# Another order for the weight splits and sums of a hybrid decoder layer: each behind the preceding split or sum alone, a room of its own for one sum, ten halves for a sum made ahead

## The chip, the cores and the metric

The kernel runs on one core of a Trainium2 chip. The metric is the device time of one execution in microseconds. Five engines work side by side, each through its own list of instructions in order: TensorE (PE, with its weight loads PEld), VectorE (DVE), ScalarE (ACT), GpSimd (POOL) and SyncE (SP, which here only starts transfers). They wait for each other through semaphores. Transfers between device memory and on-chip memory run on 16 DMA engines, which all queues share.

## The reference

The program is one decoder layer over 256 tokens with a width of 2048, all in float32. A recurrent branch and an attention branch are merged by gates (the "mix"), projected, normalised and added; then comes an MLP with a squared ReLU. The part on which this change works is the end:

```python
x = x + rmsnorm(mix @ w_out[l], norm_mix_post[l])
h = rmsnorm(x, norm_mlp_pre[l])
u = jnp.square(jax.nn.relu(h @ w_mlp_up[l]))      # 2048 -> 8192
x = x + rmsnorm(u @ w_mlp_down[l], norm_mlp_post[l])  # 8192 -> 2048
```

## The kernel before, in words

**Split weights.** A float32 product is made of three products of a shorter format: each operand is a high part plus a low part, and high x high, high x low and low x high are added. All weights are streamed once, in halves of 128 x 1024 elements (512 KB). The class `Stream` numbers them j = 8, 9, ... and takes care of three steps for each: SP loads the raw half (`wraw`, a ring of four, and every fifth half into `xraw`), ACT copies it into the high part `whi` (L108), DVE subtracts that from the raw half to get the low part `wlo` (L109). `ws.ahead` keeps the splits 6 halves ahead of PE (`AHEAD`), and the rings of `whi` and `wlo` hold 6. A ring slot of raw halves comes free only when its split is done, so DVE's order also decides when SP may load.

**The stages.** In order of time: the projections of the recurrent and the attention branch; the mix stage, whose groups alternate between a quarter of the gate (g) and a quarter of the recurrent projection (rp0 to rp3); the output projection; then twice (f = 0, 1, each half of the inner width) an up stage and two down passes (n = 0, 1, each 1024 output columns). At the end of rp0 to rp3 DVE merges the gate and both branches (L918, L919), after which PE transposes the result (L901).

**The down projection with seven products.** A down pass runs through 16 pairs of halves. For most of them (`SEVENS`) a 2 x 2 block product is made with seven block products instead of eight. Three of the seven need sums of weight blocks: `right_sums` makes them from halves a and b in three DVE instructions, L59 (T1 and T3, 1024 columns), L61 (T2, written over half of b) and L62 (T4, 512 columns). Each of T1, T3, T4 is split as well: `thi` on ACT (L154), `tlo` on DVE (L155). PE's products are all on L1191. The partial results stand in PSUM banks (s, dQ, dP, dCs). At the end of the sevens of a pass ACT and DVE combine them into four quarters (L1240 to L1244); then the last two pairs are added by plain products, and `finish` evacuates each quarter: for f = 0 by a DVE add (L1326) and a store that ACT issues (`acc_away`, L1327); for f = 1 it adds what was stored, and the last pass goes on to the norm and the output (L1366 to L1385).

**Sums made ahead.** DVE has no room for all sums in the down passes, so some are made earlier. `sums_ahead` loads a pair with four POOL transfers into `early` (L365), makes its three sums on DVE in the same three instructions, and stores them with three POOL transfers (`away`, L374); a later pass loads them back (`second`, L138). It is a generator that advances by one step for each half that PE begins, and its three gaps say how many halves pass between the loads, ahead of the sums, and between the stores. Six sums are made in the mix stage with the gaps (1, 2, 1), which is 4 + 2 + 3 = 9 halves each; eight more in the two up stages and the passes beside them.

**What sets the order.** The program is written in one stream, and a scheduler orders each engine's instructions by its own model of when they become ready. Two devices hold it: `ws.ahead`, by where it is called, and `ws.keep`. An instruction handed to `ws.keep` (all splits of pairs in the down passes, their sums and the splits of these) was given `tc.keep_in_program_order`, which keeps it behind everything that was written before it for the same engine. At the start of a new pass, the splits and sums of the first pairs are written behind the `finish` of the pass before.

**Rooms.** `pc`, `pb`, `po`, `pa` and `const` are pools of on-chip memory with different lifetimes. T1 and T3 live in a tile `t`, T4 in one of the four tiles of `u2`, a ring that the activations of the up stage and the four quarters at the end of a pass use too.

## Time and profile before

| | before |
|---|---|
| device time, median of 3 runs | 1503.71 us (1503.61 to 1503.78) |
| the profiled execution's own time | 1503.92 us |
| its span in the profile | 1502.2 us |
| granted TensorE clock, mean over the span | 0.995 |
| PE busy | 1483.7 us, 99% |
| DVE busy | 1143.2 us, 76% |
| ACT busy | 852.3 us, 57% |
| POOL busy | 77.6 us, 5% |
| read from and written to device memory | 316.38 MB, 24.64 MB |

A row of the timeline reads: start in us, duration, engine, line, operation, what is written <- what is read, and in brackets how long the engine stood idle just before and what it waited for. "SPq" and "ACTq" are the issues of transfers. A row of the windows gives the stretch, and for each engine its busy time and, in brackets, the number of instructions begun; then the granted clock of TensorE, the mean busy share of the DMA engines and the GB/s. In the chain of waits a row gives start, duration and what ran.

### The profile page before, as it was taken

What the parts mean: (1) busy time and instruction counts of PE and PEld (TensorE: products, weight loads), DVE (VectorE), ACT (ScalarE), POOL (GpSimd) and SP (SyncE); (2) the same over time, 40 slices, a digit from 0 to 9 for tenths busy, and PEclk for the clock granted to TensorE, in tenths of its full rate; (3) what the DMA queues carried; (4) which work ended last, traced back from release to release, by engine and by line L of the source; (5) the groups of instructions that cost most, each with busy time, mean ns of one, the idle gap of its engine ahead of it and who ended that gap; (6) DMA issues with size and microseconds to landing.
All of it is one profiled execution on the core that took longest, in us unless ns stands there. A gap on an engine that the chain in (4) does not pass through costs nothing.

```text
span 1502.2 us, 20543 instructions
## 1 busy us (share of the span) xinstructions
PE 1483.7 (99%) x7556; PEld 1255.6 (84%) x7556; DVE 1143.2 (76%) x1503; ACT 852.3 (57%) x1236; POOL 77.6 (5%) x149
## 2 busy tenths in 40 slices
PE   9999999999999999999999999999899999999997
PEld 8887778888889888788889888888788888888886
DVE  6676668759578966665757987799797777799897
ACT  8564564647467664444345665566465555566463
POOL 0000000000000002020000111000110111000000
PEclk9999999999999999999999999999999999999999
DMA  9754544555646658876874887668598777677584
GB/s 339 231 167 135 185 156 139 174 191 182 201 161 200 218 174 283 296 264 242 303 240 162 317 294 255 196 214 282 176 312 283 255 258 250 201 272 270 188 273 175
DMA packets 96901, 342.38 MB, mean 228 GB/s; under 512 B 11552, under 2 KB 11808, under 8 KB 95776
## 3 DMA queue, kind: packets, MB, share of 16 engines
q1 hardware_dynamic: 80352, 288.89, 57.2%
q0 software_dynamic: 12992, 44.05, 8.2%
q10 hardware_dynamic: 3456, 8.13, 1.4%
q8 instruction: 59, 0.97, 0.3%
q14 instruction: 42, 0.34, 0.1%
HBM read 316.38 MB, written 24.64 MB: 227 GB/s over the span
## 4 chain that ended last, share of the span: by engine, by line
PE 91%; DVE 4%; DMA 2%; ACT 2%; issue 1%; DVEq 0%; ACTq 0%
PE ps L296 21%; PE ps L294 11%; PE dQ L1191 7%; PE s L1191 6%; PE dP L1191 4%; PE pp L338 3%; PE pp L334 3%; PE pp L336 3%; PE g L334 3%; PE g L338 3%; PE g L336 3%; PE dCs L1191 2%; PE q L334 2%; PE q L338 2%; PE q L336 2%; PE o L336 2%
## 5 line engine op out<-in xcount | busy, mean ns | idle before, releaser
L108 ACT CAST whi<-wraw 128x1024 fp32r<-128x1024 f32 x469 | 489.3, 1051 | 464.2 <-PE ps L296 95.4
L109 DVE TENSOR_TENSOR wlo<-wraw,whi 128x1024 fp32r<-128x1024 f32 x469 | 566.8, 1220 | 243.4 <-ACT whi L108 235.2
L296 PE MATMUL ps<-h2T,whi 128*128 128x512 f32 x960 | 223.9, 390 | 0.0
L296 PEld LDWEIGHTS ps<-h2T,whi 128*128 128x128 f32 x960 | 178.2, 188 | 35.6
L294 PEld LDWEIGHTS ps<-h2T,wlo 128*128 128x128 f32 x960 | 119.1, 192 | 2.3
L296 PE MATMUL ps<-hT,whi 128*128 128x512 f32 x512 | 120.6, 391 | 0.0
L294 PE MATMUL ps<-h2T,wlo 128*128 128x256 f32 x960 | 119.9, 283 | 0.0
L296 PEld LDWEIGHTS ps<-hT,whi 128*128 128x128 f32 x512 | 94.7, 188 | 19.5 <-issue 0.7
L1191 PE MATMUL dQ<-whi,uT 128*128 128x512 f32 (+1 forms) x284 | 104.0, 385 | 0.0
L334 PE MATMUL g<-whi,hT 128*128 128x512 f32 x256 | 101.7, 397 | 0.0
L336 PE MATMUL g<-wlo,hT 128*128 128x512 f32 x256 | 100.5, 392 | 0.0
L338 PE MATMUL g<-whi,hT 128*128 128x512 f32 x256 | 100.4, 392 | 0.0
L365 POOL DMA_DIRECT2D early<-in_w_dn x56 | 30.4, 543 | 709.0 <-DVE px L324 497.9
L108 ACT CAST whi<-xraw 128x1024 fp32r<-128x1024 f32 x47 | 49.3, 1050 | 30.6 <-PE ps L296 15.2
L294 PEld LDWEIGHTS ps<-hT,wlo 128*128 128x128 f32 x512 | 63.7, 191 | 2.1 <-issue 0.8
L109 DVE TENSOR_TENSOR wlo<-xraw,whi 128x1024 fp32r<-128x1024 f32 x47 | 57.3, 1220 | 9.8 <-ACT whi L108 9.6
L294 PE MATMUL ps<-hT,wlo 128*128 128x256 f32 x512 | 64.6, 283 | 0.0
L1191 PEld LDWEIGHTS dQ<-whi,uT 128*128 128x128 f32 x284 | 53.0, 188 | 10.9 <-DVE t L1267 0.2
L1191 PE MATMUL s<-thi,uT 128*128 128x512 f32 x152 | 54.1, 397 | 4.3 <-ACT thi L154 4.3
L334 PEld LDWEIGHTS g<-whi,hT 128*128 128x128 f32 x256 | 48.5, 189 | 10.7 <-issue 1.0
L338 PEld LDWEIGHTS g<-whi,hT 128*128 128x128 f32 x256 | 48.5, 189 | 10.3
L336 PEld LDWEIGHTS g<-wlo,hT 128*128 128x128 f32 x256 | 48.4, 189 | 9.7
(309 smaller groups left out, 2750.8 us busy)
## 6 DMA issues: line engine op xcount, KB each, us to landing
wraw<-in_w_up SPq DMA_DIRECT2D x106, 512.0 KB, 4.9
wraw<-in_w_dn SPq DMA_DIRECT2D x93, 512.0 KB, 5.4
wraw<-in_w_g SPq DMA_DIRECT2D x64, 512.0 KB, 4.7
wraw<-in_w_xy SPq DMA_DIRECT2D x64, 512.0 KB, 3.7
wraw<-in_w_q SPq DMA_DIRECT2D x32, 512.0 KB, 3.8
wraw<-in_w_ap SPq DMA_DIRECT2D x32, 512.0 KB, 3.8
wraw<-in_w_rp SPq DMA_DIRECT2D x32, 512.0 KB, 5.6
wraw<-in_w_out SPq DMA_DIRECT2D x32, 512.0 KB, 4.5
```

What stands on the lines that cost most here:

```text
L108: self.pin(self.nc.scalar.copy(hi, src))
L109: self.latest_low = self.pin(self.nc.vector.tensor_tensor(lo, src, hi.bitcast(F32), ALU.subtract))
L294: mm(ps[:, f, 1, :], w, a[:, 0, :], start=False, stop=j == 1 and k == 7)
L296: mm(ps[:, f].rearrange("p a b -> p (a b)"), w, a.rearrange("p a b -> p (a b)"), start=kt == 0, stop=j == 3 and k == 7)
L334: mm(banks[tb][n], a[:, 0, t], hi[:, n * 512 : n * 512 + 512], start=first, stop=False)
L336: mm(banks[tb][n], a[:, 0, t], lo[:, n * 512 : n * 512 + 512], start=False, stop=False)
L338: mm(banks[tb][n], a[:, 1, t], hi[:, n * 512 : n * 512 + 512], start=False, stop=last)
L365: nc.gpsimd.dma_start(w[:, quarter(i)], chunks[c][:, quarter(i)])
L1191: mm(b, a[x], w[y], start=not begun and i == 0, stop=tail and i == 2, skip_group_check=shared)
```

## The change

Three edits and two small ones that make room:

1. `ws.keep` becomes `behind_latest`: a kept split or sum is ordered only behind the latest kept one on the same engine. It is no longer held behind other instructions that were written before it.
2. T4 gets a tile of its own, `t512`, in the pool `pc`, instead of one from the ring `u2`; T1 and T3 are now in `t1024`. For this `tiny` moves from `const` to `pa` and `dg` from `pb` to `po`.
3. The six sums of the mix stage take the gaps (1, 3, 1): ten halves each.

```diff
-    tiny = const.tile([P, 194], F32, name="tiny")
+    tiny = pa.tile([P, 194], F32, name="tiny")
...
-    pin = ws.pin = ws.keep = tc.keep_in_program_order
+    pin = ws.pin = tc.keep_in_program_order
+    latest = {}
+
+    def behind_latest(i):
+
+        engine = i.ins.engine
+        if engine in latest:
+            tc.add_manual_dep(i.ins, latest[engine],
+                              mybir.DependencyInfo(mybir.DependencyClass.NoSync, mybir.DependencyReason.DATA),
+                              reason="behind_latest")
+        latest[engine] = i.ins.name
+        return i
+
+    ws.keep = behind_latest
...
-    ws.side += [sums_ahead(c, (1, 2, 1), unit_rooms) for c in summed[:6]]
+    ws.side += [sums_ahead(c, (1, 3, 1), unit_rooms) for c in summed[:6]]
...
-                dg = pb.tile([P, P], F32, name=f"dg{tb}")
+                dg = po.tile([P, P], F32, name=f"dg{tb}")
...
-                ws.sums_rooms = lambda: [pc.tile([P, 1024], F32, tag="t", name="t"), u2("t4")]
+                ws.sums_rooms = lambda: [pc.tile([P, n], F32, tag=f"t{n}", name=f"t{n}") for n in (1024, 512)]
```

The changed kernel has 13 lines more, so L1326 of before is L1339 of after, and so on from line 443.

**First place: DVE in the mix stage, at the merge of rp0.** Before; the first row is L59 of the second sum made ahead, the splits are those of the last halves of rp0 and the first of the next gate quarter:

```order
L59 TENSOR_TENSOR early_t<-early 128x1024
L109 TENSOR_TENSOR wlo_5284<-wraw_5206,whi_5283 128x1024
L61 TENSOR_TENSOR early<-early_t,early 128x512
L62 TENSOR_TENSOR early_t<-early 128x512
L109 TENSOR_TENSOR wlo_5303<-wraw_5225,whi_5302 128x1024
L109 TENSOR_TENSOR wlo_5322<-wraw_5249,whi_5321 128x1024
L109 TENSOR_TENSOR wlo_5341<-wraw_5267,whi_5340 128x1024
L109 TENSOR_TENSOR wlo_5359<-wraw_5287,whi_5358 128x1024
L109 TENSOR_TENSOR wlo_5377<-wraw_5306,whi_5376 128x1024
L918 SCALAR_TENSOR_TENSOR g_4972<-g_4972,pp 128x512
L918 SCALAR_TENSOR_TENSOR g_4974<-g_4974,pp 128x512
L919 TENSOR_TENSOR g_4972<-g_4972,m_429 128x512
```

After, from the last splits before the merge:

```order
L109 TENSOR_TENSOR wlo_5340<-wraw_5267,whi_5339 128x1024
L109 TENSOR_TENSOR wlo_5359<-wraw_5285,whi_5358 128x1024
L109 TENSOR_TENSOR wlo_5377<-wraw_5305,whi_5376 128x1024
L931 SCALAR_TENSOR_TENSOR g_4972<-g_4972,pp 128x512
L931 SCALAR_TENSOR_TENSOR g_4974<-g_4974,pp 128x512
L932 TENSOR_TENSOR g_4972<-g_4972,m_429 128x512
L932 TENSOR_TENSOR g_4974<-g_4974,m_429 128x512
L109 TENSOR_TENSOR wlo_5400<-wraw_5324,whi_5399 128x1024
L109 TENSOR_TENSOR wlo_5418<-wraw_5343,whi_5417 128x1024
L59 TENSOR_TENSOR early_t<-early 128x1024
```

The second sum stands behind the merge now, and its stores and the next sum's loads stand later on POOL accordingly.

**Second place: DVE at the boundary between the two down passes of f = 0.** Before; s, dQ, dP and dCs are the banks of the ending pass, wraw_9313 and wraw_9295 the raw halves of the first pair of the next:

```order
L1243 TENSOR_TENSOR t<-t,s_8774 128x512
L1244 TENSOR_TENSOR t<-t,s_8774 128x512
L1326 TENSOR_TENSOR t<-dQ_8776,t 128x512
L1326 TENSOR_TENSOR t<-dP_8775,t 128x512
L1326 TENSOR_TENSOR t<-dQ_8777,t 128x512
L1326 TENSOR_TENSOR t<-dCs,t 128x512
L59 TENSOR_TENSOR t<-wraw_9313,wraw_9295 128x1024
L61 TENSOR_TENSOR wraw_9313<-t,wraw_9295 128x512
L62 TENSOR_TENSOR t_9465<-wraw_9313 128x512
L109 TENSOR_TENSOR wlo_9470<-wraw_9295,whi_9469 128x1024
```

After:

```order
L59 TENSOR_TENSOR t_9464<-wraw_9313,wraw_9295 128x1024
L1254 TENSOR_TENSOR t<-s_8773,t 128x512
L61 TENSOR_TENSOR wraw_9313<-t_9464,wraw_9295 128x512
L1255 TENSOR_TENSOR t<-s_8774,t 128x512
L62 TENSOR_TENSOR t_9465<-wraw_9313 128x512
L1256 TENSOR_TENSOR t<-t,s_8774 128x512
L1257 TENSOR_TENSOR t<-t,s_8774 128x512
L109 TENSOR_TENSOR wlo_9470<-wraw_9295,whi_9469 128x1024
L1339 TENSOR_TENSOR t<-dQ_8776,t 128x512
L109 TENSOR_TENSOR wlo_9474<-wraw_9313,whi_9473 128x1024
L155 TENSOR_TENSOR tlo<-t_9464,thi 128x512
L1339 TENSOR_TENSOR t<-dP_8775,t 128x512
```

The sum of the new pass and its splits moved ahead of and between the combinations and evacuations of the old one; the other two splits of sums, a further L59 and the last two evacuations follow in the same mixed way. On ACT the first copy of the new pass moved likewise from behind the four stores of L1327 to ahead of them.

**Third place: DVE at the end of the last pass.** Before, the last two splits:

```order
L1338 TENSOR_TENSOR t<-t,acc_11918 128x512
L1338 TENSOR_TENSOR t<-t,acc_11919 128x512
L1338 TENSOR_TENSOR t<-t,acc_11918 128x512
L109 TENSOR_TENSOR wlo_13246<-wraw_13133,whi_13245 128x1024
L109 TENSOR_TENSOR wlo_13250<-wraw_13176,whi_13249 128x1024
L1366 TENSOR_TENSOR acc_11918<-dQ_12659,t 128x512
```

After:

```order
L109 TENSOR_TENSOR wlo_13246<-wraw_13133,whi_13245 128x1024
L1254 TENSOR_TENSOR t<-s_12655,t 128x512
L109 TENSOR_TENSOR wlo_13250<-wraw_13176,whi_13249 128x1024
L1255 TENSOR_TENSOR t<-s_12656,t 128x512
L1351 TENSOR_TENSOR t<-t,acc_11919 128x512
```

One split stands ahead of all the combinations now, the other behind the first of them.

## The prediction

> **What bounds the kernel now.** I read the shares of the page first, then who waited for whom on PE.

> ```profile
> PE 1483.7 (99%) x7556; PEld 1255.6 (84%) x7556; DVE 1143.2 (76%) x1503; ACT 852.3 (57%) x1236; POOL 77.6 (5%) x149
> PE s L1191 <- ACT thi L154: 4.3, 1, 4.3
> PE ptr L901 <- DVE g L919: 3.6, 1, 3.6
> PE warm L440 <- DVE ones L424: 1.1, 1, 1.1
> PE s L1191 <- DVE tlo L155: 0.5, 1, 0.5
> ```

> TensorE is the bound: 99% busy. The change removes no matmul, so it can win only where PE stands still or runs slowly. Only two waits exceed 1.1 us: 3.6 before the transposes at L901 (mix stage) and 4.3 before a product of thi at L1191 (second down pass of f = 0). Both cost more than their idle time. In windows of 2 us the columns are PE busy, granted clock, DMA share, GB/s:

> ```profile
> 606.08 0.66 PE L901 MATMUL ptr<-ident,g 128*128 128x128 f32 x4 [3.61 <-DVE g L919]
> 606.00:608.00 2.00, 1.92 (x8) 0.68 0.93 367
> 608.00:610.00 2.00, 2.00 (x6) 0.50 0.76 260
> 610.00:612.00 2.00, 2.00 (x10) 0.96 0.94 332
> 1068.00:1070.00 2.00, 0.32 (x1) 0.50 0.00 0
> 1070.00:1072.00 2.00, 2.00 (x5) 0.50 0.52 145
> 1072.00:1074.00 2.00, 2.00 (x6) 0.50 0.85 260
> 1074.00:1076.00 2.00, 2.00 (x10) 0.91 0.30 123
> ```

> After each stall PE runs at half clock for some microseconds. Stall 1: 2 x (0.32 + 0.50 + 0.04) = 1.7, with the 3.6 idle **5.3 us**. Stall 2: 0.32 x 0.50 + 2 x (0.50 + 0.50 + 0.09) = 2.3, with 4.3 and the 0.5 for tlo 7.1. A second way to it is the length of the two passes, from the chain of waits:

> ```profile
> 984.78 1.36 PE s L1191 x6
> 1062.68 2.73 PE dCs L1191 x12
> 1150.57 2.72 PE dCs L1191 x12
> ```

> The first pass lasts 984.78 to 1065.41 = 80.6, the second 1065.41 to 1153.29 = 87.9. Both run the same products, so the stall costs **7.3 us**; I take this. [...]

> **Why PE waited the first time.** Rows of DVE, ACT and POOL in order of time, then the load from the chain:

> ```profile
> 588.09 1.23 DVE L59 TENSOR_TENSOR early_t<-early 128x1024 f32<-128x1024 f32 x1 [2.88 <-DMA early<-in_w_dn]
> 592.90 2.21 POOL L365 DMA_DIRECT2D early<-in_w_dn  x4 [0.18 <-issue]
> 592.94 8.88 DMA wraw<-in_w_g
> wraw<-in_w_g SPq DMA_DIRECT2D x64, 512.0 KB, 4.7
> 601.92 1.05 ACT L108 CAST whi<-wraw 128x1024 fp32r<-128x1024 f32 x1 [4.21 <-DMA wraw<-in_w_g]
> 603.00 1.23 DVE L109 TENSOR_TENSOR wlo<-wraw,whi 128x1024 fp32r<-128x1024 f32 x1 [4.04 <-ACT whi L108]
> 604.14 1.28 DVE L918 SCALAR_TENSOR_TENSOR g<-g,pp 128x512 f32<-128x512 f32 x2
> 605.34 1.28 DVE L919 TENSOR_TENSOR g<-g,m 128x512 f32<-128x512 f32 x2
> ```

> The transposes need the merge L918/L919. It stands on DVE behind a split whose raw half took 8.88 us to arrive, against a median of 4.7. Two things delayed that half. DVE had waited 2.88 us at 588.09 for the data of a sum made ahead, so ring slots came free late; and POOL put the four loads of the next sum on the DMA engines at 592.90, in the same moment as the late half, with this sum's stores just ahead.

> ```profile
> 580.00:600.00 20.00, 20.00 (x90) 16.57 (x89) 11.81 (x12) 9.02 (x10) 5.76 (x11) 1.00 0.90 309
> 600.00:620.00 20.00, 16.39 (x70) 13.15 (x70) 14.42 (x16) 8.60 (x10) 3.47 (x7) 0.91 0.91 326
> 700.00:720.00 20.00, 20.00 (x96) 16.40 (x95) 12.60 (x14) 8.95 (x10) 0.00 (x0) 1.00 0.64 221
> ```

> **Part 1, ten halves.** The gap (1,2,1) -> (1,3,1) lets each sum take ten halves instead of nine. On DVE the second sum's L59 goes from ahead of six splits before the merge to the third place behind it; its stores and the next loads follow on POOL. Before the merge DVE loses one L59 (1.23), one L61 and one L62 (0.69 each, L61's shape as in the L1326 rows below) and the wait of 2.88: about 5.5 us. The late half is then asked for some 3 to 4 us earlier and without 1.25 MB of stores and 1 MB of loads beside it. If it takes the 4.7, the merge ends near 599.5 (an estimate: half at 594 to 595, split and casts 2.3, merge 2.6). PE's last matmul before the wait ended at 606.08 - 3.61 = 602.5, so the margin is about 3 us. Gain between 0 (half still late) and 5.3; I take 5.3, since 3 us of margin covers most of the 8.88 - 4.7 = 4.2 of lateness even if it recurs. The moved traffic, some 2.25 MB, lands in 600 to 622 on top of 326 GB/s; the next merge lies at about 640, behind a quiet stretch, and the sums further back fall near 700, where the DMA share was 0.64.

> **Part 2, the order of splits and sums.** Rows at the boundary of the passes:

> ```profile
> 1044.92 0.33 SPq L86 DMA_DIRECT2D wraw<-in_w_dn  x1
> 1050.77 20.56 SPq L86 DMA_DIRECT2D wraw<-in_w_dn  x4
> 1049.52 2.58 DVE L109 TENSOR_TENSOR wlo<-wraw,whi 128x1024 fp32r<-128x1024 f32 x2 [0.37 <-ACT whi L108]
> 1057.27 0.69 DVE L1326 TENSOR_TENSOR t<-dQ,t 128x512 f32<-128x512 f32 x1 [1.33 <-PE dQ L1191]
> 1065.43 0.69 DVE L1326 TENSOR_TENSOR t<-dCs,t 128x512 f32<-128x512 f32 x1 [2.03 <-PE dCs L1191]
> 1066.04 1.22 DVE L59 TENSOR_TENSOR t<-wraw,wraw 128x1024 f32<-128x1024 f32 x1
> 1066.53 1.04 ACT L108 CAST whi<-wraw 128x1024 fp32r<-128x1024 f32 x1 [13.42 <-DVE t L1326]
> 1085.47 6.93 DMA wraw<-in_w_dn
> ```

> The sum L59 of the next pass's first pair stood behind four evacuations, which wait for PE to end the pass; ACT's first copy waited 13.42 us behind the stores of those evacuations. PE reached 1065.4 with nothing split. After, a kept split or sum is bound only to the kept one before it. DVE's work to the first pair's last tlo is then 3 instructions of 1024 columns (1.22) and 11 of 512 (0.69), the four combinations and two evacuations among them: 3.7 + 7.6 = 11.3 us from 1049.52 + 2.58 = 1052.1, so at most 1063.4. PE comes at 1065.4, so 2 us are left over. The inputs are there: half 369 was issued at 1044.92, and the slowest down load of the chain took 6.93. Ring slots come free earlier too, where SP's four issues took 20.56 us before, and that removes the 0.5 at tlo, whose load was the late one of 1085.47. The price is that evacuations now stand behind splits. The one wanted first is dQ of the quarter (0,0), whose bank the third product of the new pass writes, 6 matmuls x 0.227 (2.72 / 12) = 1.4 us after 1065.4. By the same count DVE reaches it at 1063.4 + 1.22 and is done 0.69 later, at 1065.3: 1.5 us are left, so I count nothing, and 0.7 if DVE were 2 us later than counted. Gain 0 to 7.3; I take 7.3, as the pass before it, which starts with splits in hand, loses nothing. The boundary of f = 1 showed no wait before, and keeps at most 1.2 us (one split) in either direction; I count it at nothing, the end of its pass being hidden under PE.

> **Part 3, the end.** The last two splits pass eight small DVE instructions, so PE's dQ products need not be put off:

> ```profile
> 1485.58 0.47 PE dQ L1191 x2
> 1492.52 0.61 DVE acc L1366
> 1494.64 0.34 DVE acc L1366
> 1493.50 0.28 PE L1191 MATMUL s<-whi,uT 128*128 128x256 f32 x1
> ```

> The chain leaves PE at 1486.05 and stays on DVE and ACT to the last accumulation at 1494.64, while PE ends at 1493.78. With dQ complete some 3 us earlier DVE catches up and the tail hangs on PE: 1494.64 - 1493.78 = 0.86 less an issue, **0.75** (bounds 0 and 0.86).

> **Part 4, rooms.** A room of its own for the third sum frees u2; `tiny` and `dg` only change pools. No row shows a wait on them; nothing. One raw load early in the up stage moves behind four others on SP; its half is needed over 15 us later: nothing, or at worst one wait of a load, 6.9 less the lead.

> **Sum.** Against the profiled execution's 1503.92: 1503.92 - 5.3 - 7.3 - 0.75 = 1490.6. The median of the runs is 0.2 lower, which I leave to the thin margin named under rival C: **1490.6 us**.

> **The rivals.** *B, stall 1 moves.* The traffic of the sums is moved, not removed; a merge or the first group of rp1 to rp3 may meet a late half instead. For it: 0.90 DMA share over 40 us. Against it: DVE is busy 12 to 14 of 20 us there, so it catches up after a late half if no merge stands right behind it. Price 5.3: 1495.9.

> *C, DVE becomes the bound in places.*

> ```profile
> 1100.00:1120.00 20.00, 20.00 (x90) 16.57 (x89) 19.93 (x24) 15.06 (x21) 1.62 (x3) 1.00 0.84 292
> ```

> In a down pass DVE is busy 19.93 of 20 us, so whatever it does at a boundary is paid for later. The second pair of the new pass needs its first tlo after the 21 matmuls of the first pair and 12 of its own that use plain splits, at 1065.4 + 33 x 0.227 = 1072.9; DVE reaches it, counted on from 1063.4 (at full durations) with five of 1.22 and five of 0.69, at 1072.95. By the steps between neighbours (603.00 to 604.14, 1.14; 1065.43 to 1066.04, 0.61) both counts end some 2 us earlier. So the margin is 2.0 to -0.1. Three or four waits of up to 1 us give 1493.5.

> *D, slower.* A kept sum now stands on DVE and ACT ahead of evacuations; if its raw half is late, everything behind it in the engine's queue waits, and PE with it for a bank, as L918 stood ready behind a split that waited 4.04. [...] A late load as at 1085.47 gives a stall of some 4.3 idle and 2.3 at half clock, 6.6. It decides from the third such place on (2 x 6.6 is what is gained): three boundaries of down passes at 6.6 give 1490.6 + 19.8 = 1510. Against it: at the boundary seen, the halves were issued over 7 us ahead.

> *E, nothing changes.* Both waits come back, as the same DVE work meets the same late halves: 1503.7. Against it: DVE idles 1.33 and three times 2.03 at the boundary, which is time to use.

> **How the numbers follow.** Forecast A 0.62 (own range 1489.0 to 1492.0), B 0.14, C 0.13, D 0.07, E 0.04. The range starts at 1488.5, which is 1490.6 less the 0.1 that the tail may bring above 0.75, the 1.2 of a split at the boundary of f = 1, the 0.2 by which the median lies lower and 0.6 for the two half-clock stretches, which differ by that much from each other; it ends at 1497.0, B's 1495.9 with about 1 us of C's waits. It holds A, C and B and leaves out D and E. Below 0.2% (3.0 us) a measurement of this kernel can't be told from no change; A, B and C are faster by more: 0.89; E same: 0.04; D slower: 0.07.

> **What would show it.** In the changed profile: no wait at the transposes of the mix stage and granted clock 1.00 from 600 to 620 (part 1); the second pass of f = 0 near 80.6 long, L59 of its first pair at about 1052, and no wait for thi (part 2); the last accumulation right behind PE's last matmul (part 3). A wait of PE over 3.5 us anywhere, with half clock behind it, or short waits for tlo summing to over 2 us, would make the forecast wrong.

## The result and the profile after

The changed kernel takes 1489.01 us (median of 5 runs, 1488.93 to 1489.47); the kernel before, beside it, 1503.61. The ratio of the means is 0.9908, 95% interval 0.9894 to 0.9923. The profiled execution took 1488.93 with a span of 1487.0. One run of the kernel before (3422.96) and one of e4 (3251.23) took more than twice as long as all others and are left out of every figure below. The forecast was 1490.6: right in direction and in its three places, 1.6 us short in size.

The chain on the page by engine, and then who waited for whom on PE:

```profile
PE 97%; DVE 1%; ACT 1%; DMA 0%; issue 0%; DVEq 0%; ACTq 0%
```

```profile
PE warm L440 <- DVE ones L424: 1.1, 1, 1.1
PE kv L476 <- ACT hT L460: 0.4, 1, 0.4
PE pt L693 <- DVE s L677: 0.2, 1, 0.2
```

Both long waits and the 0.5 for tlo are gone, and PE's share of the chain is 97% (91% before). The windows of 20 us at the two places show PE busy throughout at full clock:

```profile
600.00:620.00 20.00, 20.00 (x93) 16.56 (x93) 13.70 (x16) 9.07 (x11) 4.34 (x8) 1.00 0.80 291
1060.00:1080.00 20.00, 20.00 (x90) 16.54 (x89) 17.62 (x20) 11.70 (x17) 3.23 (x6) 1.00 0.94 330
```

The chain gives the lengths of the two down passes of f = 0:

```profile
978.82 1.36 PE s L1204 x6
1056.34 2.72 PE dCs L1204 x12
1136.58 2.72 PE dCs L1204 x12
```

They last 978.82 to 1059.06 and 1059.06 to 1139.30, 80.24 each, against 80.6 and 87.9. Setting the same instructions of both traces side by side shows where the 15.2 us lie by which the span is shorter:

| stretch | before | after | gain |
|---|---|---|---|
| start to the matmul before the first transposes of the mix stage | 602.08 | 601.63 | 0.45 |
| from there to the first down pass | 382.70 | 377.19 | 5.5 |
| f = 0, first pass | 80.63 | 80.24 | 0.4 |
| f = 0, second pass | 87.88 | 80.24 | 7.6 |
| up stage and first pass of f = 1 | 258.73 | 258.73 | 0.0 |
| f = 1, second pass to PE's last matmul | 81.76 | 81.30 | 0.5 |
| from there to the end | 8.42 | 7.67 | 0.75 |

DVE at the merge in the mix stage, at the pass boundary and at the end; behind it PE's row of the first transposes:

```profile
592.66 2.53 DVE L109 TENSOR_TENSOR wlo<-wraw,whi 128x1024 fp32r<-128x1024 f32 x2 [4.38 <-ACT whi L108]
600.15 1.29 DVE L932 TENSOR_TENSOR g<-g,m 128x512 f32<-128x512 f32 x2
603.63 1.22 DVE L59 TENSOR_TENSOR early_t<-early 128x1024 f32<-128x1024 f32 x1
...
1045.68 1.22 DVE L59 TENSOR_TENSOR t<-wraw,wraw 128x1024 f32<-128x1024 f32 x1
1054.49 1.28 DVE L155 TENSOR_TENSOR tlo<-t,thi 128x512 fp32r<-128x512 f32 x2
1064.24 1.89 DVE L155 TENSOR_TENSOR tlo<-t,thi 128x512 fp32r<-128x512 f32 x3
...
1479.35 0.42 DVE L1379 TENSOR_TENSOR acc<-s,t 128x256 f32<-128x256 f32 x1 [1.08 <-PE s L1204]
```

```profile
601.87 0.60 PE L914 MATMUL ptr<-ident,g 128*128 128x128 f32 x4
```

The merge ends at 601.44, and PE takes it up at 601.87: only 0.4 us to spare, since late halves of weights (4.38 us of waiting at 592.66) are still there, only earlier. The last half before the merge, issued at 592.94 in the kernel before, is now issued and copied here:

```profile
588.31 0.33 SPq L86 DMA_DIRECT2D wraw<-in_w_g  x1
596.73 1.06 ACT L108 CAST whi<-wraw 128x1024 fp32r<-128x1024 f32 x1 [0.55 <-DMA wraw<-in_w_g]
```

It is asked for 4.6 us earlier, but it still takes 8.3 us to land (8.88 before); two of POOL's loads for a sum made ahead are issued beside it here too, at 588.21 and 588.77. What the changed kernel gained is the earlier request and not a faster transfer.

At the boundary the first pair's last tlo is done at 1055.77, 3.3 us before PE needs the pass to begin at 1059.06. At the end DVE now waits 1.08 us for PE, where before PE's results had waited for DVE.

### The profile page after: what moved, and what is told of

Read it like the earlier page. It is cut to its first block, busy times and chain, and to the rows that moved or that the text cites. A ratio compares the mean times of both kernels' runs of the same rounds, so it can differ in the third digit from the quotient of the medians.

```text
span 1487.0 us, 20528 instructions
## 1 busy us (share of the span) xinstructions
PE 1477.6 (99%) x7556; PEld 1253.4 (84%) x7556; DVE 1144.4 (77%) x1503; ACT 854.8 (57%) x1236; POOL 77.5 (5%) x149
## 4 chain that ended last, share of the span: by engine, by line
PE 97%; DVE 1%; ACT 1%; DMA 0%; issue 0%; DVEq 0%; ACTq 0%
PE ps L296 22%; PE ps L294 11%; PE dQ L1204 8%; PE s L1204 7%; PE dP L1204 4%; PE g L334 4%; PE g L336 4%; PE pp L334 4%; PE g L338 4%; PE pp L336 4%; PE pp L338 4%; PE dCs L1204 2%; PE q L334 2%; PE q L338 2%; PE q L336 2%; PE o L336 2%
## 5 line engine op out<-in xcount | busy, mean ns | idle before, releaser
L109 DVE TENSOR_TENSOR wlo<-wraw,whi 128x1024 fp32r<-128x1024 f32 x469 | 566.6, 1220 | 245.4 <-ACT whi L108 242.9
L108 ACT CAST whi<-wraw 128x1024 fp32r<-128x1024 f32 x469 | 489.9, 1051 | 452.4 <-PE ps L296 92.9
L108 ACT CAST whi<-xraw 128x1024 fp32r<-128x1024 f32 x47 | 49.4, 1052 | 40.7 <-PE ps L296 18.4
L109 DVE TENSOR_TENSOR wlo<-xraw,whi 128x1024 fp32r<-128x1024 f32 x47 | 57.3, 1219 | 12.1 <-ACT whi L108 11.2
L365 POOL DMA_DIRECT2D early<-in_w_dn x56 | 30.4, 543 | 651.9 <-DVE px L324 497.6
L1204 PE MATMUL dQ<-wlo,uT 128*128 128x512 f32 (+1 forms) x142 | 54.6, 385 | 0.0
## 6 DMA issues: line engine op xcount, KB each, us to landing
wraw<-in_w_up SPq DMA_DIRECT2D x106, 512.0 KB, 4.5
wraw<-in_w_dn SPq DMA_DIRECT2D x93, 512.0 KB, 5.0
wraw<-in_w_g SPq DMA_DIRECT2D x64, 512.0 KB, 4.7
wraw<-in_w_xy SPq DMA_DIRECT2D x64, 512.0 KB, 3.9
wraw<-in_w_q SPq DMA_DIRECT2D x32, 512.0 KB, 4.1
wraw<-in_w_ap SPq DMA_DIRECT2D x32, 512.0 KB, 3.9
wraw<-in_w_rp SPq DMA_DIRECT2D x32, 512.0 KB, 5.3
wraw<-in_w_out SPq DMA_DIRECT2D x32, 512.0 KB, 4.4
```

The lines of the kernel that those rows point to most:

```text
L108: self.pin(self.nc.scalar.copy(hi, src))
L109: self.latest_low = self.pin(self.nc.vector.tensor_tensor(lo, src, hi.bitcast(F32), ALU.subtract))
L365: nc.gpsimd.dma_start(w[:, quarter(i)], chunks[c][:, quarter(i)])
L1204: mm(b, a[x], w[y], start=not begun and i == 0, stop=tail and i == 2, skip_group_check=shared)
```

## The experiments

All times are medians. The kernel before, run beside e1 to e4, took 1503.24, beside e5 to e8 1501.05 and beside the last three 1502.54; its runs spread over up to 5.6 us, those of the changed kernel over 0.5, so differences are taken to the changed kernel's 1489.01. The changed kernel was not run again beside the experiments; e6 and e10, which have the same two stalls removed, came to 1489.46 and 1489.12, so differences of medians below some 0.5 us mean nothing.

**Each part by itself.** The first takes back the gap, the second the order, the third the room; the fourth puts the gap alone into the kernel before.

```diff
-    ws.side += [sums_ahead(c, (1, 3, 1), unit_rooms) for c in summed[:6]]
+    ws.side += [sums_ahead(c, (1, 2, 1), unit_rooms) for c in summed[:6]]
```

> The changed kernel (1489.0) with the gaps of the six sums put back to (1, 2, 1), nine halves. Theory (the gap alone removes the wait at the transposes): the second sum stands ahead of the merge again, so the wait of 3.6 us and the 1.7 at half clock come back, 1494.3 to 1494.6, and the second down pass of f = 0 stays at 80.2. Rival (the new order of splits is what freed the mix stage, or both are needed): 1489.0 with no wait there, or a second pass longer than 81.

Measured 1493.07 (1491.12 to 1493.78), 4.1 above the changed kernel. The wait is back, shorter, and in the profiled execution no half clock follows it:

```profile
604.19 0.66 PE L914 MATMUL ptr<-ident,g 128*128 128x128 f32 x4 [2.17 <-DVE g L932]
```

```profile
604.00:606.00 2.00, 1.81 (x10) 1.00 1.02 397
606.00:608.00 2.00, 2.00 (x11) 1.00 0.82 303
```

That execution took 1491.12, the fastest of the five; the other four took 1492.73 to 1493.78. So, in the changed kernel, the gap alone decides on the wait, but its price is not fixed: 2.2 here, 5.5 in the profile before.

```diff
-    ws.keep = behind_latest
+    ws.keep = tc.keep_in_program_order
```

> The changed kernel with kept splits and sums in program order again (ten halves and the room for the third sum stay). Theory (the order alone removes the wait at the pass boundary): second pass of f = 0 at 87 to 88 again, the tail 0.75 longer: 1489.0 + 7.6 + 0.75 = 1497.4, up to 1498.2 if the small waits of the other passes (0.4 each) return too; no wait at the transposes of the mix stage. Rival (the room of the third sum did it): below 1491.

Measured 1497.46 (1496.90 to 1499.12), as the theory said, except that PE also waits 0.3 at the transposes of the mix stage, where it forecast none. From the chain, then from the waits:

```profile
1057.24 2.73 PE dCs L1204 x12
1144.08 2.72 PE dCs L1204 x12
```

```profile
PE s L1204 <- ACT thi L154: 4.3, 1, 4.3
```

The wait of 4.3 at the boundary is the same as before. The second pass lasts 1059.97 to 1146.80 = 86.8; that is 6.6 of the 8.4. Most of the rest is the tail and the small waits of the first pass and the last one, which return too (the first pass is 80.63 long again, as before).

```diff
-                ws.sums_rooms = lambda: [pc.tile([P, n], F32, tag=f"t{n}", name=f"t{n}") for n in (1024, 512)]
+                ws.sums_rooms = lambda: [pc.tile([P, 1024], F32, tag="t1024", name="t1024"), u2("t4")]
```

> The changed kernel with T4 in the ring u2 again. Theory (the room is worth little: the third sum waits for the store of the first evacuated quarter, and the first tlo is ready within 0.3 us of PE's need): 1489.0 to 1490. Rival (the room is needed, since the ring's four tiles are held by the four quarters at the boundary): the first tlo comes over 3.5 us late, half clock follows, 1494 to 1497.

Measured 1490.61 (1490.39 to 1491.80): 1.6 above the changed kernel, between the two. Rows of DVE at the boundary, and PE's only wait for a tlo:

```profile
1054.24 0.69 DVE L1339 TENSOR_TENSOR t<-dP,t 128x512 f32<-128x512 f32 x1 [2.03 <-PE dP L1204]
1054.85 0.68 DVE L62 TENSOR_TENSOR t<-wraw 128x512 f32<-128x512 f32 x1
1060.73 1.21 DVE L59 TENSOR_TENSOR t<-wraw,xraw 128x1024 f32<-128x1024 f32 x1
```

```profile
1083.28 0.50 PE L1204 MATMUL s<-tlo,uT 128*128 128x512 f32 x1 [0.83 <-DVE tlo L155]
```

Without the room L62 stands behind two evacuations, with DVE idle in between, and the next pair's L59 begins at 1060.73 instead of 1055.69. The first pair is still in time, but the debt comes due 20 us later. A later half is asked for at 1073.49 instead of 1070.28 (0.6 of it lost before this pass), and the product of tlo at 1083.28 follows the one of thi 1.22 us on, 1.0 more than the usual 0.227. In all the second pass is 81.55 long, 1.3 more than in the changed kernel. With the room the place is thin too (e10 loses 0.1 there and e11 0.4), but not by that much. So the room has a price of its own, and it is paid a pair or two further on than both theories had it. This profiled execution also lost some 0.5 further up, in small waits that come and go (see the end of e11).

```diff
-    ws.side += [sums_ahead(c, (1, 2, 1), unit_rooms) for c in summed[:6]]
+    ws.side += [sums_ahead(c, (1, 3, 1), unit_rooms) for c in summed[:6]]
```

> The kernel before with the gaps (1, 3, 1) alone. Theory (the two gains are independent and add up): 1503.6 - 5.4 = 1498.2, second pass of f = 0 still 87 to 88. Rival (they depend on each other): 1503.6 when the order is needed for it, or a second pass of another length.

Measured 1498.93 (1498.23 to 1500.32), 4.3 below the kernel before (1503.24 beside it). The wait at the transposes is gone, and the second pass is 88.9, longer than forecast, in the slowest of the runs, which is the one that was profiled. With e1 to e3: 4.1 for the gap, 8.4 for the order, 1.6 for the room, 14.1 of the 14.6 measured; the parts add up.

e4 differs from e2 by the room alone (with `tiny` and `dg`) and is 1.5 slower. Both keep the old order, and from the first L59 of the second pass to 1083 DVE does the same work in the same order, 0.4 us apart. What differs is when POOL loads stored sums back into `second`. These rooms come from the ring u2 as well (the kernel sets `ws.room = u2`), which the description of the rooms above does not say. First e4, with the load of a half from its chain of waits, then e2:

```profile
1079.38 1.79 POOL L138 DMA_DIRECT2D second<-away  x3 [0.15 <-DMA wraw<-away]
1080.40 7.94 DMA wraw<-in_w_dn
```

```profile
1055.27 0.54 POOL L138 DMA_DIRECT2D second<-away  x1 [26.18 <-DVE t L1339]
```

With T4 in the ring, these loads stand on POOL behind loads into `early` and are issued just ahead of the late half, which takes 7.94 us; PE then waits 0.6 for thi and 0.8 for tlo. With the room they are issued between 1055.27 and 1061.77, the same half, issued at 1080.04, takes 5.1, and PE does not wait. The kernel before has the same picture: these loads at 1084.70, a half issued at 1085.47 that takes 6.93, and the wait of 0.5 for tlo. That the loads beside the half made it late is read from these traces; no run holds them back by themselves. In e3 they stand beside the half of 1073.49 as well, but it takes 6.7 us against 7.2 in the changed kernel, so there it is the later request that counts.

**Which sum matters.** Ten halves for the first two sums only:

```diff
+    ws.side += [sums_ahead(c, (1, 3 if i < 2 else 2, 1), unit_rooms) for i, c in enumerate(summed[:6])]
```

> The changed kernel with ten halves for the first two sums only, nine for the other four. Theory (all that counts is that the second sum passes the merge of rp0): 1489.0, no wait at the transposes. Rival (the later sums collide elsewhere at nine halves): a wait in rp1 to rp3, over 1490.5.

Measured 1489.46 (1488.68 to 1490.05), with no wait there. With the gap of nine halves the later four sums cost nothing that shows; the first two carry the gain.

**Why the half was late.** The first run did not move the loads:

```diff
+    six = [sums_ahead(c, (1, 2, 1), unit_rooms) for c in summed[:6]]
+    ws.side += six[:2] + [iter([None] * 4)] + six[2:]
```

> The changed kernel at nine halves again (1493.1 measured), with a pause of five halves between the second and the third sum made ahead: the second sum's L59 keeps its place ahead of the merge and its wait for data, its stores keep theirs, only the third sum's four loads leave the moment of the late half. Theory (the loads crowd the late half on the DMA engines): the wait at the transposes falls below 1 us, 1489.0 to 1490.2. Rival (the half is late because DVE's wait for the sum holds up the ring slot, or because of the stores): the wait stays at 2 us or more, 1491.2 or more.

Measured 1491.25, wait 1.8. But POOL's four loads were still issued at 590.54, right behind the stores: a load that waits for nothing was not held back by being written later. Only the fourth sum's two loads had left. The next two hold POOL for good, by a copy of one column of a later split's `wlo`:

```diff
+    def behind_split():
+        cells.append(pa.tile([P, 1], F32, name=f"cell{len(cells)}"))
+        return nc.gpsimd.tensor_copy(cells[-1], ws.parts[ws.split - 1][1][:, 0:1].bitcast(F32))
...
+            held.enter_context(tc.issue_after(behind_split().ins))
         for i in range(4):
             nc.gpsimd.dma_start(w[:, quarter(i)], chunks[c][:, quarter(i)])
```

> The changed kernel at nine halves, where the third sum's four loads are now really held: POOL first copies one column of a split that lies behind the merge, and the loads stand behind that copy. DVE's order up to the merge, the wait of the second sum for its data and its stores are those of nine halves (e1: 1493.1, wait 2.2). Theory (the third sum's loads are what makes the half late): wait below 0.5, 1489.0 to 1489.8. Rival 1 (the stores are enough): wait about 2, 1491 to 1493. Rival 2 (the half is asked for late, as the second sum's wait held up DVE): as rival 1, and the same in the next run.

> As before, and the second sum's three stores are held behind the merge too. Theory (crowded DMA engines): no wait at the transposes, 1489.0 to 1489.6. Rival 2 (the half is asked for late): wait about 2 with nothing of POOL's beside it, 1491 to 1493.

In e10 the second sum's three stores stand behind such a copy as well. Measured: loads held 1491.66 (1490.55 to 1493.06), both held 1489.12 (1488.99 to 1489.82). DVE's order up to the merge is the same in both. The timeline of the loads held, then of both held: the second sum's L59, a store of POOL, ACT's copy of the late half and the first row of the merge:

```profile
588.37 1.23 DVE L59 TENSOR_TENSOR early_t<-early 128x1024 f32<-128x1024 f32 x1 [4.37 <-DMA early<-in_w_dn]
592.46 0.54 POOL L393 DMA_DIRECT2D away<-early_t  x1 [0.18 <-issue]
600.15 1.05 ACT L108 CAST whi<-wraw 128x1024 fp32r<-128x1024 f32 x1 [3.69 <-DMA wraw<-in_w_g]
602.37 1.28 DVE L950 SCALAR_TENSOR_TENSOR g<-g,pp 128x512 f32<-128x512 f32 x2
```

```profile
588.06 1.22 DVE L59 TENSOR_TENSOR early_t<-early 128x1024 f32<-128x1024 f32 x1 [3.94 <-DMA early<-in_w_dn]
596.94 1.05 ACT L108 CAST whi<-wraw 128x1024 fp32r<-128x1024 f32 x1 [2.15 <-DMA wraw<-in_w_g]
599.16 1.28 DVE L950 SCALAR_TENSOR_TENSOR g<-g,pp 128x512 f32<-128x512 f32 x2
608.57 1.08 POOL L393 DMA_DIRECT2D away<-early_t  x2
```

DVE waits some 4 us for the second sum in both, and the half is issued at about the same time, at 593.22 and 592.91. With the stores (1.25 MB) out of the way it takes 3.93 us instead of 6.83 and is copied at 596.94 instead of 600.15, and PE does not wait. So the stores suffice to make the half late, and the loads beside them need not be there (whether the loads alone would do it was not run). That the half is asked for late is not enough by itself; nor is a slow transfer, since the changed kernel's takes 8.3 us. The wait needs both, and either cure removes it: nine halves with the stores held is as fast as ten.

**What a wait costs.** Two and four extra DVE instructions on the merged gate (its maximum with itself) at the end of rp0:

```diff
+        for _ in range(2 if n == 0 else 0):
+            nc.vector.tensor_tensor(gs[0], gs[0], gs[0], ALU.max)
         waiting.append(merge(n, gs))
```

> The changed kernel with two more DVE instructions on the merged gate (its maximum with itself) at the end of rp0, so that PE waits some 1.9 us at the transposes by the order on DVE. Theory (a wait of that length costs itself alone): 1490.9, granted clock 1.00 behind it. Rival (half clock follows every wait of microseconds): 1.7 to 2.3 more, 1492.6 to 1493.2.

> The same with four such instructions, which makes a wait of some 5.4 us. Theory (a wait as long as the two in the kernel before halves the clock behind it for 1.7 to 2.3 us of loss): 1489.0 + 5.4 + 2.0 = 1496.4. Rival (the half clock there had another cause, such as crowded DMA engines or the boundary): 1494.4, granted clock 1.00.

Measured 1491.78 (1490.27 to 1493.62) and 1490.69 (1489.96 to 1493.89). The long wait did not come about: the order moved the transposes some 3.4 us back behind other matmuls of the next group, and PE waited 1.7, as against 1.4 in the short one; so e8 tests neither its theory nor its rival. Neither profiled execution shows a clock below 1.00. But the runs of both spread over 3 to 4 us. And in the run with the loads held, a wait of 2.1 is followed by half clock (e9, in the slowest of its four runs; the wait, then windows as in the prediction):

```profile
PE ptr L933 <- DVE g L951: 2.1, 1, 2.1
```

```profile
604.00:606.00 2.00, 1.69 (x8) 0.75 0.63 199
606.00:608.00 2.00, 2.00 (x6) 0.50 0.46 133
608.00:610.00 2.00, 2.00 (x9) 0.89 0.89 258
```

Eight matmuls there start 0.427 us apart instead of 0.227, and the one ahead of them 0.32, a loss of 1.7. In e1 a wait of 2.2 at the same place cost nothing more; the last section sets the two side by side.

**The end.** Program order again for f = 1 alone:

```diff
     for f in range(2):
         uT = {}
         rooms = []
         if f:
+            ws.keep = tc.keep_in_program_order
```

> The changed kernel with program order again for the kept splits and sums of f = 1 only. Theory (the tail's 0.75 is a gain of its own, and the small waits of the last pass add 0.4): 1489.0 + 0.75 to 1.2 = 1489.8 to 1490.2, the chain ending on DVE from the first evacuation on. Rival (the tail gains nothing, what it shows is stalls further up): 1489.0.

Measured 1491.14 (1489.82 to 1491.28), 2.1 above the changed kernel and more than expected. The profiled execution splits it. The rows of the chain, of the changed kernel and then of this one:

```profile
1395.31 2.72 PE dCs L1204 x12
1477.16 2.17 PE s L1204 x18
```

```profile
1396.51 2.72 PE dCs L1204 x12
1476.93 2.74 DVE x L1399 x4
1481.79 0.34 DVE acc L1380
```

From the end of the first pass of f = 1 to the end of the span it takes 1399.23 to 1489.3 = 90.1 instead of 1398.03 to 1487.0 = 89.0: 1.1, within the forecast, and the chain runs over DVE as before. The other 1.2 lies ahead of that point. Of it 1.1 is lost by 1083, where both programs still have the same instructions in the same order: at a wait for u at 823 (the next product comes 0.65 later than in the changed kernel) and at one for tlo (0.43), where the changed kernel has none:

```profile
PE ps L296 <- DVE u L1146: 0.4, 1, 0.4
PE s L1204 <- DVE tlo L155: 0.2, 1, 0.2
```

Such waits come and go between executions of one program order; why, the traces don't show. They set the limit to what a single profile of these kernels tells, about 1 us.

## Why the prediction was right, point by point

**Part 1, ten halves.** Forecast 5.3, in the two traces 5.5, in the medians 4.1 to 4.3. That the gap of the first two sums decides was shown (e1, e4, e6). Both causes named for the late half are real and the wait needs both (e9, e10 and the changed kernel's own trace); of the traffic the stores suffice, while the prediction named the loads and the stores alike. Of its two gains only the first came: the half is asked for 4.6 us earlier, but the transfer was not freed and took 8.3 us where the estimate let it take the median of 4.7. So the margin is 0.4 us and not 3. That the term held all the same is luck to that extent: any margin above zero saves the whole price, and with half a microsecond less there is a wait again, as the 0.3 in e2 shows.

**Part 2, the order.** Forecast 7.3 for the second pass, measured 7.6, of which e2 gives 6.6 to the order. The rest is the wait for tlo, which belongs to the room (part 4), and the clock: the stall had 6.8 us of half clock in the profile before and some 3.5 in e2 (an estimate from the mean granted clock from 1060 to 1080, 0.83 before and 0.91 in e2). The margins came out wider than counted at full durations: 3.3 us where 2.0 was given, and for the second pair's first tlo (1064.92, wanted at 1066.5) 1.6 in the bounds -0.1 to 2.0. Rival C, small waits through a dense DVE, did not come: DVE was busy 17.62 of 20 us from 1060. The passes that were counted at nothing brought 0.4 and 0.5: in the first and the last pass a few products, among them the first of a tlo, start some 0.1 us late; this returns with program order (e2), so "loses nothing" was not quite true of the pass before.

**Part 3, the end.** Forecast 0.75, measured 0.75, and the last accumulation hangs on PE.

**Part 4, the room.** This is the step that failed: "nothing", measured 1.6 (e3), of which 1.3 lie in the second pass of f = 0 of its profile, and 1.5 between e2 and e4 (1497.46 and 1498.93), where the order is the old one. That no row showed PE or DVE waiting for `u2` was not enough: the ring's price appears as an order. With the new order (e3) L62 stands behind the evacuations that free its tile; with the old one (e4 and the kernel before) the loads into `second` come late and beside an urgent half. The trace before had the consequence, the 0.5 for tlo at 1095; the prediction saw the late load of 1085.47 behind it, but booked it under the order, and it is the room that removes it (it is gone in e2 and 0.8 in e4).

**The sum** was 1.6 too high in time. In the spans the gain is 15.2 and the terms add up to 13.35; the difference of 1.85 is 0.45 by which PE was ahead at 602 already, 0.2 in stall 1, 0.3 in the second pass, and 0.4 and 0.5 in the two passes counted at nothing. The room's price is no part of it, since its effect on the kernel before was in the 7.3. Rival D (hoisted sums that hold up the evacuations) did not come: the halves of the new pass were in time.

## What to carry to other kernels

Look for waits of the bounding engine and price each by the time that the next stage begins, not by the idle time, since the half clock behind it added half as much again here (1.7 us to 3.6 idle, 2.3 to 4.3). At a boundary between passes, work for the next pass that is held behind evacuations by program order alone cost 6.6 us of a pass here; bind it only to what it depends on, and give it room that the evacuations don't hold. Look up everything that lives in a shared ring: here transfers of another engine hung on it. A load or store made "ahead" was not free here where an urgent load shared the DMA engines with it (the late half took 6.83 us with the stores beside it in e9, 3.93 without them in e10; 7.94 with loads of stored sums beside it in e4, 5.1 without in e2), and writing loads later did not hold them back (e5, still issued at 590.54).

## What the runs showed of the hardware

Waits of about the same length were not always followed by half clock: 2.2 us of waiting left the clock at 1.00 (e1), and so did 1.4, 1.7 and 1.8 (e7, e8, e5), while 2.1 at the same place was followed by 3.4 us at 0.50 (e9). The four profiled waits of 3.6 and 4.3 all came with half clock: 3.4 us of it at stall 1 and 6.8 at stall 2 in the kernel before, and a mean granted clock of 0.91 from 1060 to 1080 in e2 and in e4, at their waits of 4.3.

```profile
603.31:606.73 3.42, 0.65 (x5) 1.00 1.03 402
606.73:610.14 3.41, 3.41 (x10) 0.50 0.81 293
1064.11:1067.52 3.41, 1.28 (x6) 1.00 0.36 136
1067.52:1070.94 3.42, 1.26 (x3) 0.50 0.10 26
1070.94:1074.35 3.41, 3.41 (x8) 0.50 0.83 261
599.90:603.31 3.41, 2.57 (x12) 1.00 1.00 389
```

```profile
600.06:603.47 3.41, 1.96 (x9) 1.00 1.02 408
603.47:606.88 3.41, 2.69 (x14) 1.00 0.95 366
```

```profile
601.60:605.01 3.41, 1.28 (x8) 1.00 0.64 216
605.01:608.43 3.42, 3.42 (x9) 0.50 0.46 144
```

In e1 the end of a stretch cuts the wait in two, and neither stretch is idle for more than 43%; that its stretches lie just there is the author's reading, which no row here shows. In e9 the wait lies in one stretch, which is idle for 62%, and the next one runs at half clock. In the kernel before the stretches that were idle for 81% (stall 1), 62% and 63% (stall 2, two in a row) were each followed by one at 0.50, and the one ahead of stall 1, idle for 25%, by one at 1.00. That the idle share of a stretch decides on the clock of the next one is read from these few; no run varies it by itself. Half clock cost 1.7 us at stall 1 and in e9, half of 3.4, and 2.3 at stall 2, where PE was busy for 1.26 + 3.41 of the 6.8 us at 0.50.

If that reading holds, a kernel with a wait of 2 to 4 us can pay for half clock in one run and not in the next. The runs of most kernels with such a wait do spread over more: 2.1 to 3.9 us for e1, e2, e4, e7, e8 and e9, against 0.5 to 1.5 for the changed kernel, e3, e6, e10 and e11, which have none; e5, with a wait of 1.8 and a spread of 0.7, does not fit. Only one run of each was profiled, so that the clock makes this spread is not shown.
